# Layer 0's output projection as seven products of half size, on one core

## The chip, the cores and the metric

The kernel runs on one core of one Trainium2 chip. The metric is the device time of one execution in microseconds (us). Before the change the median of three runs is 2584.62 us (2582.84 to 2584.84). One core has TensorE (PE; its weight loads are listed apart as PEld), VectorE (DVE), ScalarE (ACT), GpSimd (POOL) and SyncE (SP), which issues nearly all DMAs of this kernel.

## The reference

One sequence of S = 1024 rows and D = 1024 columns in fp32 goes through two layers. Layer 0 mixes by dilated attention, layer 1 by gated linear attention, and each is followed by a squared-ReLU MLP, with an RMSNorm ahead of every part.

```python
DILATED_GROUPS = ((128, 1), (512, 4), (2048, 16))
for i in range(DEPTH):                     # 2
    h = rmsnorm(x, norm_mix_w[i])
    x = x + (dilated_attention if i % 2 == 0 else gla_mixer)(h, ...)
    h = rmsnorm(x, norm_mlp_w[i])
    x = x + sq_relu_mlp(h, mlp_w_up[i], mlp_w_down[i])
return rmsnorm(x, final_norm_w)
```

The dilated attention has 8 heads of 128 columns and three groups; a group's output is joined with the others by softmax weights. Its last step is `o @ w_out`, a product of 1024 x 1024 by 1024 x 1024, added to x. That step is the subject here.

## The kernel before, in words

**Products in three parts.** A product in fp32 is made of three matmuls in a faster format (fp32r): each operand is split into hi and lo, and hi·hi, hi·lo and lo·hi are summed in PSUM (`mm3`, L195 to L198). A split costs a copy on ScalarE (hi) and a subtraction on VectorE (lo). The large products ahead of the projection are done with seven products of half-size blocks in place of eight (names a11, s1 to s4, a22 and so on, L841); the output projection is not.

**The heads.** The stage that runs from 247 to 855.4 us makes, for 24 pairs (head, group) with number p = 0 to 23, the projection to q, k and v (L841), the rotation (L1309 to L1317), scores, masks, exponentials and the product with v. The three groups come in turn. Classes (L1234 to L1272) is the code of the third group, Attention (L1158 to L1209) that of the other two. The attention of pair p runs while pair p + 1 is projected. The order is written as an agenda: `at(t, fn, rank)` puts a function at step t, a pair has 14 steps, and the functions of one step run by rank. Every engine takes its instructions in the order in which these functions write them. Outputs of the groups go to DRAM (og), and the merge of a head loads them as rows (L1379), weighs them (L1386 to L1395), and joins them into om (L1403, L1404), which goes to DRAM as oscr.

**The projection (the crossing).** `out_proj(0, ...)` (L1713 on) turns rows of the heads' output into columns (`turned.turn`, pT L259; `t_head`, pT L1447), splits them (oTh, oTl, o1h, o1l), splits the rows of w_out (raw, whi, wlo: L133, L152, L153), and makes 8 blocks of 128 rows by 2 halves of the columns by 8 parts of k by 3: 384 matmuls of 128x512 into pd (L196 to L198). The first half of k (heads 0 to 3) is done for all rows first, while the attention of pair 23 and the merge of head 7 still run between; those are the steps of `tail()`, one or two to each `tick()`. Each block is added to x in the tile xs (L1732), and the norm of the MLP (L214 to L242) and its first products follow (pX, pY, L841).

**Buffers and queues.** Tiles come from rings: k4 has slots of 4 KB to a partition and h8 slots of 8 KB. A writer waits for the last reader of the slot that it takes. All the loads and stores of this stage are in SyncE's queue: one that waits (for a buffer or for a result) holds those behind it.

Of the kernel before, what the change touches and what calls it, by code (L numbers as in the profile page):

```python
# [19 lines left out]
P = 128  # L20
# [17 lines left out]
RAW = 4  # L38
# [3 lines left out]
def hybrid_trunk(ctx, tc, x, norm_mix, norm_mlp, norm_fin, a_in, a_out, g_in, g_up, g_b, g_nw,  # L42
# [67 lines left out]

    class Weights:
        def __init__(self):
            self.slots = []
            self.ndma = 0
            self.nprep = 0
            self.used = 0
            self.freed = 0
# [62 lines left out]
    def add_rows(w, k0):  # L180
        for k in range(2):
            W.add(w[P * (k0 + k):P * (k0 + k + 1), :])
# [79 lines left out]
    class Split:  # L262
# [19 lines left out]
    class Halves:  # L282
# [374 lines left out]
    class Trickle:  # L657
# [73 lines left out]

        step = Ahead.step

    def up_columns(i):
        return lambda p, k: [(0, cols(m_up[i], 256 * p, 256, 4 * k, 4))]

# [10 lines left out]
    class Up:  # L747
# [217 lines left out]
    zscr, gscr, uscr = (drp.tile([S, D], F32, name=n) for n in ("zscr", "gscr", "uscr"))  # L965
    wpre = [[[drp.tile([P, 1024], F32, name=f"wp{i}_{p}_{n}") for n in PARTS] for p in range(AHEAD)] for i in range(3)]

    wout = [tuple(drp.tile([P, D], F32, name=f"wo{k}_{n}") for n in range(2)) for k in range(KT)]
    gnw = masks[:, 132:134]

# [430 lines left out]
    def merge_join(rows, eng):  # L1401
        o = t2([P, 4, HD], F32, "om")
        eng.tensor_tensor(o, rows[:, :, 0, 0:HD], rows[:, :, 1, 0:HD], op=OP.add)  # L1403
        eng.tensor_tensor(o, o, rows[:, :, 2, 0:HD], op=OP.add)  # L1404
        return o

    def merge(rows, d, e, z):
        merge_shares(rows, d, e, z)
        o12 = rows.rearrange("p t g c -> p (t g) c")[:, :, 0:HD]
        dve.tensor_tensor(o12, o12, e.rearrange("p t g -> p (t g)").unsqueeze(2).to_broadcast([P, NG * 4, HD]),  # L1410
                          op=OP.mult)
        return merge_join(rows, dve)

    def merges(h, done):

        rows, part = {}, {}

        def load(half):
            rows[half] = merge_load(h, half)

        def start(half):
            part[half] = merge_weights(rows[half])

        def finish(half):
            done(h, half, merge(rows.pop(half), *part.pop(half)))
        return load, start, finish

    oT1 = {}

# [11 lines left out]
    def t_head(h, half, o):  # L1441

        kp, k = divmod(h - 4, 2)
        hi, lo = second(half, kp)
        ps = bank("pT")
        for b in range(4):
            pe.transpose(ps[:, 128 * b:128 * b + 128], o[:, b, :], ident)  # L1447
        split(hi[:, k, :], lo[:, k, :], ps)

    reached = set()  # L1450

    def merged(h, half, o):
        if h < HEADS - 1:
            sp.dma_start(oscr[512 * half:512 * half + 512, HD * h:HD * h + HD].rearrange("(b p) c -> p b c", p=P), o)
        else:
            def last():
                t_head(h, half, o)
                reached.add((0, half))
            at(336 + (28, 34)[half], last)

    def ahead_h8(pairs):

        t = h8([P, 4, 512], F32, "ol")
        sp.dma_start(t, oscr[512 * pairs:512 * pairs + 512, 0:512].rearrange("(b p) c -> p b c", p=P))
        return [t[:, 0:2, :], t[:, 2:4, :]]

    def plan_merges(h, c):

        rows, part = {}, {}

        def load(half):
            rows[half] = merge_load(h, half)

        def weigh(half):
            part[half] = merge_weights(rows[half])

        def join(half):
            del part[half]
            merged(h, half, merge_join(rows.pop(half), dve))
        for half in range(2):  # L1480
            t = c + 9 + 11 * half
            at(t, lambda half=half: load(half))
            if half and h == HEADS - 2:
                t += 9
# [4 lines left out]
            at(t + 10, lambda half=half: join(half), 9)  # L1489


    x0 = []
# [163 lines left out]
    ol = []  # L1656
    turned = Turned(ol, x[0])
    for p in range(heads.count):
        h, g = divmod(p, NG)
        if g == 1 and h:  # L1660
            plan_merges(h - 1, 14 * p)
        if p == heads.count - 1:
            for k in range(0, KT, 2):
                add_rows(a_out, k)
            c = 14 * p
            at(c + 3, lambda: (ol.extend(ahead_h8(0)), W.dma(), W.dma()), 0)
            at(c + 4, lambda: (W.dma(), W.dma()), 0)
            for t in (6, 8, 9, 10):
                at(c + t, lambda: W.prep(dve), 7)
            at(c + 8, lambda: turned.turn(0), 7)  # L1670
            at(c + 9, lambda: (turned.load_x(0), turned.load_x(1)))
            at(c + 11, lambda: turned.turn(1), 7)
        heads.run_head(p)

    def drain_to(mark):
        while mark not in reached:
            steps.popleft()()
            now[0] += 1
            run_due()

    def tail():

        c = clock[0]
        heads.follow(heads.count - 1, c, ((7, 7, 8, 8), (11, 11, 12, 12), (13, 13, 14, 14)))
        ol.extend(ahead_h8(1))
        load, start, finish = merges(HEADS - 1, merged)
        rows = {}

        def early(half):
            t = rows[half] = h8([P, 4, 512], F32, "ol2")  # L1690
            sp.dma_start(t[:, :, 0:384], oscr[512 * half:512 * half + 512, 512:896].rearrange("(b p) c -> p b c", p=P))

        def turn(half, h):
            t_head(h, half, rows[half][:, :, HD * (h - 4):HD * (h - 4) + HD])

        def weights():
            W.early = RAW
        at(c + 1, lambda: early(0))
        at(c + 8, weights)
        at(c + 14, lambda: early(1))  # L1700
        for t, half, h in ((10, 0, 4), (12, 0, 5), (14, 0, 6), (22, 1, 4), (24, 1, 5), (26, 1, 6)):
            at(c + t, lambda half=half, h=h: turn(half, h))
        at(c + 16, lambda: (load(0), load(1)), 9)
        for half, t in ((0, 22), (1, 26)):
            at(c + t, lambda half=half: start(half), 9)
        for half, t in ((0, 24), (1, 28)):
            at(c + t, lambda half=half: finish(half), 9)
        steps.extend([advance] * 44)

    tail()  # L1710


    def out_proj(layer, wbc_row, o, up):  # L1713
# [783 lines left out]
```

## Time and profile before

| what | value |
|---|---|
| median of 3 runs | 2584.62 us (2582.84 to 2584.84) |
| the profiled execution | 2582.79 us, of which the span is 2581.0 |
| granted clock of TensorE | 0.999 |
| DMA moved | 544.33 MB, mean 211 GB/s |

All instants are us from the start of the span. A row of a timeline has start, duration, engine, line, operation, output and inputs, count, and in brackets how long the engine was idle before it and what ended that. In a row by stretches the values are the stretch, its length, busy us (instructions) of PE, PEld, DVE, ACT and POOL, the granted clock, the mean busy share of the 16 DMA engines and GB/s. L numbers are lines of the kernel before, unless said otherwise.

### The profile page before, as it was taken

The numbers are of one execution on the slowest core, as the hardware profiler recorded it, in microseconds if no ns is written. First come the engines' busy times: TensorE is split into PE (matmuls) and PEld (weight loads), VectorE is DVE, ScalarE is ACT, GpSimd is POOL, SyncE is SP. The second block draws the span as 40 slices with busy tenths as digits, with TensorE's granted clock in tenths as the row PEclk, the third lists the DMA queues.
The fourth block names the chain that finished last, engine by engine and source line by source line (L and its number), as shares of the span: only waits on it lengthen the run. The fifth ranks groups of instructions, "written<-read, shape, count | busy, mean of one in ns | idle before, by whom it ended". The sixth has DMA issues, their size and how long they took to land.

```text
span 2581.0 us, 34661 instructions
## 1 busy us (share of the span) xinstructions
PE 2565.0 (99%) x12586; PEld 2120.0 (82%) x12586; DVE 1864.6 (72%) x3000; ACT 1283.6 (50%) x2344; POOL 20.2 (1%) x24
## 2 busy tenths in 40 slices
PE   9999999999999999999999999999999999999998
PEld 6888888888888888888888888888888888888887
DVE  7766788888888766788668795687666666666666
ACT  6443455555545435666544453554335555553344
POOL 0000000000000000000000000110000000000000
PEclk9999999999999999999999999999999999999999
DMA  5785456656565846799798865777445644495543
GB/s 176 243 279 193 108 147 153 157 143 169 141 167 148 270 165 246 263 336 337 265 329 286 288 214 194 271 238 290 171 165 194 237 161 136 147 349 200 189 146 125
DMA packets 357708, 544.33 MB, mean 211 GB/s; under 512 B 25536, under 2 KB 181568, under 8 KB 357536
## 3 DMA queue, kind: packets, MB, share of 16 engines
q1 hardware_dynamic: 357392, 541.85, 64.3%
q8 instruction: 99, 1.62, 0.3%
q14 instruction: 73, 0.60, 0.1%
q10 hardware_dynamic: 144, 0.26, 0.0%
HBM read 338.93 MB, written 177.93 MB: 200 GB/s over the span
## 4 chain that ended last, share of the span: by engine, by line
PE 88%; DVE 4%; ACT 4%; DMA 2%; issue 2%; SPq 0%; DVEq 0%; ACTq 0%
PE pX L841 16%; PE pB L1858 13%; PE pV L841 11%; PE pA L1858 10%; PE pB L1051 8%; PE pA L1051 5%; PE pY L841 5%; PE pZ L841 5%; PE pd L196 2%; PE pd L198 2%; PE pd L197 2%; PE pO L1199 1%; PE pS L1158 1%; PE pT L259 1%; PE pP L1185 1%
## 5 line engine op out<-in xcount | busy, mean ns | idle before, releaser
L1858 PE MATMUL pB<-dh 128*128 128x512 f32 x512 | 199.2, 389 | 0.0
L1858 PE MATMUL pB<-dl,dh 128*128 128x512 f32 x512 | 199.2, 389 | 0.0
L1858 PE MATMUL pB<-dh,dl 128*128 128x512 f32 x512 | 199.2, 389 | 0.0
L205 DVE TENSOR_TENSOR dl<-sin,dh 128x1024 fp32r<-128x1024 f32 x112 | 136.8, 1221 | 62.2 <-ACT dh L202 59.3
L841 PE MATMUL pV<-s4h,wd 128*128 128x512 f32 x480 | 161.4, 398 | 0.6 <-DVE qk L2054 0.4
L202 ACT ACTIVATE dh<-sin 128x1024 fp32r<-128x1024 f32 x112 | 117.8, 1052 | 78.8 <-PE pB L1858 29.8
L1858 PE MATMUL pA<-dh 128*128 128x512 f32 x384 | 149.6, 390 | 0.0
L1858 PE MATMUL pA<-dh,dl 128*128 128x512 f32 x384 | 149.4, 389 | 0.0
L1858 PE MATMUL pA<-dl,dh 128*128 128x512 f32 x384 | 149.4, 389 | 0.0
L846 ACT ACTIVATE e<-pX 128x512 f32<-128x512 f32 x108 | 64.4, 596 | 155.2 <-PE pX L841 155.1
L202 ACT ACTIVATE dh<-kept 128x1024 fp32r<-128x1024 f32 x64 | 67.8, 1060 | 145.1 <-DVE kept L1823 102.0
L779 DVE TENSOR_TENSOR wbl<-t,wbh 128x1024 fp32r<-128x1024 f32 x48 | 58.8, 1226 | 78.7 <-ACT wbh L778 78.7
L1858 PEld LDWEIGHTS pB<-dh,dl 128*128 128x128 f32 x512 | 96.1, 188 | 20.0
L1858 PEld LDWEIGHTS pB<-dh 128*128 128x128 f32 x512 | 96.1, 188 | 20.0
L1858 PEld LDWEIGHTS pB<-dl,dh 128*128 128x128 f32 x512 | 96.1, 188 | 19.8
L841 PEld LDWEIGHTS pV<-s4h,wd 128*128 128x128 f32 x480 | 90.1, 188 | 20.5 <-DVE qk L2054 0.8
L1174 ACT ACTIVATE pt<-pt,orow 128x256 f32<-128x256 f32 (+1 forms) x128 | 59.8, 468 | 91.0 <-DVE orow L1172 87.3
L841 PE MATMUL pX<-s3h,wgh 128*128 128x512 f32 x240 | 96.8, 403 | 0.0
L841 PE MATMUL pX<-s2h,wbh 128*128 128x512 f32 x240 | 96.0, 400 | 0.2
L841 PE MATMUL pV<-s1h,wbh 128*128 128x512 f32 x240 | 95.6, 398 | 0.0
L841 PE MATMUL pY<-a12h,wah 128*128 128x512 f32 x240 | 95.3, 397 | 0.0
L841 PE MATMUL pX<-a11h,wah 128*128 128x512 f32 x240 | 95.0, 396 | 0.0
(370 smaller groups left out, 7251.7 us busy)
## 6 DMA issues: line engine op xcount, KB each, us to landing
sin<-acts SPq DMA_DIRECT2D x112, 512.0 KB, 4.4
acts<-s SPq DMA_DIRECT2D x64, 512.0 KB, 3.5
raw<-in_mlp_w_down_dram SPq DMA_DIRECT2D x64, 512.0 KB, 5.3
raw<-in_attn_w_in_dram SPq DMA_DIRECT2D x96, 256.0 KB, 4.5
cw<-c SPq DMA_DIRECT2D x192, 128.0 KB, 2.3
raw<-in_mlp_w_up_dram SPq DMA_DIRECT2D x48, 512.0 KB, 5.9
acts<-c SPq DMA_DIRECT2D x64, 256.0 KB, 3.0
kept<-in_mlp_w_down_dram SPq DMA_DIRECT2D x32, 512.0 KB, 6.4
```

The lines of the kernel that those rows point to most:

```text
L196: pe.matmul(ps, sh, mh, start=start, stop=False)
L197: pe.matmul(ps, sh, ml, start=False, stop=False)
L198: pe.matmul(ps, sl, mh, start=False, stop=stop)
L202: act.activation(hi, src, AF.Copy)
L205: dve.tensor_tensor(lo, src, hi.bitcast(F32), op=OP.subtract)
L259: pe.transpose(ps[e][:, 64 * n:64 * n + 64], src[k, :], ident[k, k], tile_position=(64 * e, 0))
L779: self.remain(lambda: dve.tensor_tensor(lo, src, hi.bitcast(F32), op=OP.subtract))
L841: pe.matmul(st[b], u[:, k, :], v, start=first and k + n == 0, stop=k == 3 and n == 2, skip_group_check=True)
L846: act.activation(e, self.st[p]["X"], AF.Copy)
L1051: pe.matmul(self.acc[s][t], a[:, c], b[:, k, :], start=fresh and m + k + v == 0, stop=m == 1 and k == 1 and v == 2, skip_group_check=True)
L1174: act.activation(pt[:, i, :128 * n], pt[:, i, :128 * n], AF.Exp, scale=-1.0, bias=m, accum_out=self.row[:, r, HD:HD + 1])
L1858: pe.matmul(self.acc[s][t], a[:, k, c], b[:, k, :], start=fresh and m + k + v == 0, stop=m == 7 and k == 1 and v == 2, skip_group_check=True)
```

## The change

**The products.** The projection of 1024 x 1024 by 1024 x 1024 is cut into blocks of half the size (rows, k and columns in two halves), and done by seven products of 512 x 512 by 512 x 512. The sums of the left operand's blocks are a11, a22, a12, s1 to s4; those of the weights are b11, b21, b22, t1 to t4. There are seven times four blocks (of 128 rows) with four parts of k and three matmuls each. They accumulate in three groups in PSUM: Q (b11, t3, t4), Z (t2, t1, b22), and R (b21). A group is added to xs at one or two places when it holds the right partial sum.

**The weights.** The class `OutParts` makes the weights' sums and splits them beside the heads, in eight plans of four steps each: a plan loads two pieces of w_out (256 KB each), makes four differences of 256 columns, seven splits (three of two pieces together, one of one), and stores hi and lo of the seven in DRAM, in 14 stores of 128 KB. A step runs at t = 7 and t = 14 of a pair, at t = 7 alone if p is a multiple of 3, from p = 1 on, last in its step's rank. All plans are done by p = 20. In pair 23 and the projection they are loaded back: seven sums of four loads, 512 KB each, one load per step of the agenda. The splits of w_out beside the projection (8 on ScalarE, 8 on VectorE) are gone, as are oTl and o1l.

**The agenda.** The sums and splits of the heads' output stand at steps of pair 23 and of `tail()`. The second half of the merge of head 6 is weighed earlier and joined later, straight into the tile that the projection reads.

The core of the diff:

```diff
+        def plan(self, k, cols):
...
+            def cut(i, *names):
...
+                act.activation(hi, src, AF.Copy)
+                def rest():
+                    dve.tensor_tensor(lo, src, hi.bitcast(F32), op=OP.subtract)
+                    for j, name in enumerate(names):
+                        for m, to in enumerate(self.out[name]):
+                            sp.dma_start(to[:, k, cols], both[:, m, j, :].bitcast(F32))
+                self.behind.append(rest)
+            def less(to, a, b):
+                t = r["t"]
+                dve.tensor_tensor(t[:, to, :], t[:, a, :], t[:, b, :], op=OP.subtract)
...
         if p == heads.count - 1:
-            for k in range(0, KT, 2):
-                add_rows(a_out, k)
...
+        elif p:
+            for t in ((7,14), (7,))[p % 3 == 0]:
+                at(14 * p + t, parts.step, 9)
...
+        for t0, name in ((12, "t2"), (18, "t1"), (33, "b22"), (37, "b21")):
+            plan += [(t0 + i, fn) for i, fn in enumerate(proj.load(name))]
...
+        whole("Q", "b11", "a11", True, (1, 0), (1, 1))
+        whole("Q", "t3", "s3", False, (0, 1))
+        for t in range(4):
+            pr.product("Q", "t4", "a22", t, ks)
...
+        whole("Z", "t1", "s1", False, (0, 1))
...
-    out_proj(0, norm_mlp[0], turned, up)
+    project(norm_mlp[0], up)
```

Three places show what it moves. The first is VectorE where pair 12 begins, from the difference of two weight blocks (t, from raw) to the rotation: c is a projected column block, pt the masked scores, cw the swapped half of c. Before:

```order
L815 TENSOR_TENSOR t<-raw 128x512
L816 TENSOR_TENSOR t<-raw,t 128x512
L1300 TENSOR_TENSOR c<-pZ,e_5013 128x512
L1172 ISA pt,orow<-pS,masks 128x128
L1172 ISA orow 128x1
L1172 ISA pt,orow<-pS,masks 128x256
L1172 ISA orow 128x1
L1309 TENSOR_TENSOR cw<-cw,tab 128x512
```

The same place after the change, where wpc is the tile of a split of OutParts:

```order
L954 TENSOR_TENSOR t<-raw 128x512
L955 TENSOR_TENSOR t<-raw,t 128x512
L763 TENSOR_TENSOR wpc<-raw,wpc 128x512
L771 TENSOR_TENSOR raw<-raw 128x256 x2
L1440 TENSOR_TENSOR c<-pZ,e_5157 128x512
L1312 ISA pt,orow<-pS,masks 128x128
L1312 ISA orow 128x1
L1312 ISA pt,orow<-pS,masks 128x256
L1312 ISA orow 128x1
L1449 TENSOR_TENSOR cw<-cw,tab 128x512
```

A split of 512 elements and two differences of 256 stand ahead of the block and of all that follows it in the queue. The second place is VectorE in the crossing, from the last rotation of pair 23 (qT) to the first masks of Classes (pt from pS). Before:

```order
L1317 TENSOR_TENSOR qT<-c,cw 128x16x32
L1732 TENSOR_TENSOR xs<-pd,xs 128x512
L1386 TENSOR_REDUCE mz<-rows 128x4
L1387 TENSOR_TENSOR md<-mz,rows 128x12
L1392 TENSOR_TENSOR md<-me,rows 128x12
L1393 TENSOR_REDUCE mz<-md 128x4
L1394 RECIPROCAL mz<-mz 128x4
L1395 TENSOR_TENSOR me<-me,mz 128x12
L1732 TENSOR_TENSOR xs<-pd,xs 128x512
L1244 ISA pt,orow<-pS,masks 128x64
```

After, where ap are the blocks and sums of the left operand, and s3h and s3l their split:

```order
L871 TENSOR_TENSOR xs<-pQ,xs 128x512 x2
L855 TENSOR_TENSOR ap<-ap 128x4x256
L1449 TENSOR_TENSOR cw<-cw,tab 128x512
L1450 TENSOR_TENSOR c<-c,tab 128x512
L1457 TENSOR_TENSOR qT<-c,cw 128x16x32
L850 TENSOR_TENSOR s3l<-ap,s3h 128x2x256 x2
L871 TENSOR_TENSOR xs<-pQ,xs 128x512 x2
L855 TENSOR_TENSOR ap<-ap 128x4x256
L850 TENSOR_TENSOR s3l<-ap,s3h 128x2x256 x2
L871 TENSOR_TENSOR xs<-pQ,xs 128x512 x2
L1384 ISA pt,orow<-pS,masks 128x64
```

The merge's weights (mz to me) have moved ahead of qT, and sums, splits and adds stand around it. The third place is TensorE where the joined first half of head 7 (om) is turned. Before, after 168 matmuls into pd:

```order
L196 MATMUL pd<-whi,oTh 128x512
L197 MATMUL pd<-wlo,oTh 128x512
L198 MATMUL pd<-whi,oTl 128x512
L1447 MATMUL pT<-ident,om 128x128 x4
L196 MATMUL pd<-whi,oTh 128x512
```

After, in the product of t2 by s2:

```order
L865 MATMUL pZ<-wph,s2h 128x512
L865 MATMUL pZ<-wpl,s2h 128x512
L865 MATMUL pZ<-wph,s2l 128x512
L836 MATMUL pT<-ident,om 128x128 x4
L865 MATMUL pZ<-wph,s2h 128x512
```

The turn of om stands 18 matmuls earlier, after 132 matmuls into pQ and 18 into pZ; the other matmuls between are the same in number.

More of the change, by code (lines that the diff above doesn't have):

```diff
@@ L732, in hybrid_trunk, with __init__, load, one @@
         step = Ahead.step
+    class OutParts:
+        NAMES = ("b11", "t1", "t3", "t2", "b21", "b22", "t4")
+        def __init__(self, w, out):
+            self.w, self.out = w, out
+            self.todo, self.behind = deque(), deque()
+            for k in range(4):
+                for half in range(2):
+                    self.plan(k, slice(256 * half, 256 * half + 256))
+        step = Ahead.step
+        def plan(self, k, cols):
+            r = {}
+            def load():
+                t = r["t"] = k4([P, 4, 256], F32, "raw")
+                for i in range(2):
+                    row = P * (k + 4 * i)
+                    sp.dma_start(t[:, 2 * i:2 * i + 2, :],
+                                 self.w[row:row + P, :].rearrange("p (a c) -> p a c", a=2)[:, :, cols])
+            def cut(i, *names):
+                n = len(names)
+                both = k4([P, 2, 2, 256], F32R, "wpc")
+                hi, lo, src = both[:, 0, :n], both[:, 1, :n], r["t"][:, i:i + n, :]
+                act.activation(hi, src, AF.Copy)
[8 more added lines that the diff above has]
+                dve.tensor_tensor(t[:, to, :], t[:, a, :], t[:, b, :], op=OP.subtract)
+            def one():
+                less(1, 1, 0)
+                cut(0, "b11", "t1")
+            def two():
+                cut(2, "b21", "b22")
+                less(1, 3, 1)
+                less(0, 1, 0)
+            def three():
+                cut(0, "t3", "t2")
+                less(2, 2, 1)
+            def four():
+                cut(2, "t4")
+            if self.todo:
+                last = self.todo.pop()
+                self.todo.append(lambda: (last(), load()))
+            else:
+                self.todo.append(load)
+            self.todo.extend((one, two, three, four))
@@ L1422, in start, with scale @@
             part[half] = merge_weights(rows[half])
+        def scale(half, n):
+            if not n:
+                merge_shares(rows[half], *part[half])
+            merge_scale(rows[half], part[half][1], n)
         def finish(half):
-            done(h, half, merge(rows.pop(half), *part.pop(half)))
-        return load, start, finish
+            r, p = rows.pop(half), part.pop(half)
+            done(h, half, merge_join(r, dve) if half else merge(r, *p))
+        return load, start, finish, scale
     oT1 = {}
@@ L1455, in merged @@
         else:
[L1456 to L1459, printed above, removed]
+            LAST[half] = o
     def ahead_h8(pairs):
@@ L1478, in join @@
             del part[half]
[L1479 removed]
+            if h == HEADS - 2 and half:
+                merge_join(rows.pop(half), dve, LAST["ol"][:, :, 2 * HD:])
+            else:
+                merged(h, half, merge_join(rows.pop(half), dve))
         for half in range(2):
@@ L1679, in drain_to @@
             run_due()
+    while parts.todo or parts.behind:
+        parts.step()
     def tail():
@@ L1693, in turn @@
[L1693 to L1705, printed above, removed]
@@ L1706, in tail, with turn @@
-        for half, t in ((0, 24), (1, 28)):
-            at(c + t, lambda half=half: finish(half), 9)
-        steps.extend([advance] * 44)
-    tail()
+            t = rows[half] = h8([P, 4, 384], F32, "ol2")
+            n = 384 - 128 * half
+            if half:
+                LAST["ol"] = t
+            sp.dma_start(t[:, :, :n], oscr[512 * half:512 * half + 512, 512:512 + n].rearrange("(b p) c -> p b c", p=P))
+        def turn(half, k):
+            proj.head(NAMES[half], k, rows[half][:, :, HD * k:HD * k + HD] if k < 3 else LAST[half])
```

219 lines of the change are left out of this document (196 added, 23 removed).

## The prediction

> **What bounds the kernel now.** I read the page first (part 1, the busy shares; part 4, the chain that ended last), then the busy time by stretches, then the chain and the engines' timelines inside the stretch that the change rewrites.
>
> ```profile
> PE 2565.0 (99%) x12586; PEld 2120.0 (82%) x12586; DVE 1864.6 (72%) x3000; ACT 1283.6 (50%) x2344; POOL 20.2 (1%) x24
> ...
> PE 88%; DVE 4%; ACT 4%; DMA 2%; issue 2%; SPq 0%; DVEq 0%; ACTq 0%
> ```
>
> TensorE is never idle to speak of, and the chain lies on it for 88%: a matmul that goes away is worth its time, as long as nothing else is late behind it. What else could be late is read by stretches (each row: PE, PEld, DVE, ACT, POOL busy, clock, DMA share, GB/s). One row for the heads first; the others run from the end of the last head into the output projection, which starts at 855.4; I call that instant T = 0.
>
> ```profile
> 320.00:855.40 535.40, 534.48 (x3084) 447.07 (x3083) 450.80 (x970) 297.43 (x807) 0.00 (x0) 1.00 0.62 158
> ```
> ```profile
> 833.00:843.00 10.00, 9.80 (x69) 8.19 (x67) 7.44 (x10) 6.15 (x14) 0.00 (x0) 1.00 0.99 310
> 843.00:855.40 12.40, 12.40 (x76) 10.24 (x77) 10.90 (x21) 7.99 (x18) 0.00 (x0) 1.00 1.02 302
> 855.40:869.40 14.00, 14.00 (x77) 11.57 (x77) 11.52 (x26) 4.28 (x14) 0.00 (x0) 1.00 0.89 278
> 869.40:885.00 15.60, 15.60 (x145) 12.85 (x144) 9.07 (x31) 11.96 (x39) 0.00 (x0) 1.00 0.86 253
> 885.00:900.00 15.00, 15.00 (x84) 12.28 (x83) 8.69 (x17) 2.94 (x6) 0.00 (x0) 1.00 0.91 271
> 900.00:915.00 15.00, 14.83 (x69) 11.68 (x68) 13.73 (x22) 3.19 (x5) 0.00 (x0) 1.00 0.11 36
> ```
>
> And from the chain of waits (start, duration, what):
>
> ```profile
> 833.32 7.92 DMA raw<-in_attn_w_out_dram
> ```
>
> Two things count. VectorE is busy for 450.8 of 535.4 us of the heads (84%), so work put beside them meets little slack. And from 833 to 900 the DMA engines are 86 to 102% busy: the last line is a load of output weights that is itself on the chain. The change adds to both.
>
> **The matmuls that go.** Two groups of twelve 128x512 matmuls on the chain:
>
> ```profile
> 958.63 2.72 PE pX L841 x12
> 961.35 2.72 PE pY L841 x12
> ```
>
> 2.72 / 12 = 0.227 us each (the groups' mean of 389 ns overlaps the next matmul). 384 of them become 28 x 12 = 336: 48 x 0.227 = **-10.9 us**. The splits of the weights that held TensorE between 900 and 915 go too: 15.00 - 14.83 = **-0.2**. The clock is 1.00 in every row; I keep it.
>
> **The crossing: the waits that come.** The profile shows none of the new waits; I bound them by counting what stands in the queues. First VectorE ahead of Classes' scores (the last head's third group):
>
> ```profile
> 866.85 1.04 DVE L1317 TENSOR_TENSOR qT<-c,cw 128x512 f32<-128x512 f32 x1
> ...
> 868.42 0.15 DVE L1386 TENSOR_REDUCE mz<-rows 128x4 f32<-128x12 f32 x1
> ...
> 869.70 0.17 DVE L1395 TENSOR_TENSOR me<-me,mz 128x12 f32<-128x12 f32 x1
> ...
> 875.44 0.22 DVE L1244 CUSTOM_DVE_ANT_0 pt<-pS,masks 128x64 f32<-128x64 f32 x1
> ```
> ```profile
> 869.41 1.08 PE pS L1234 x32
> ...
> 877.30 0.44 PE pP L1254 x4
> ```
>
> Before, qT was done at T = 12.5 and its scores came at 14.0. The next rows price one VectorE instruction by the start of the next one: 1.14 us for 1024 elements (559.46 to 560.60), 0.6 for 512 (561.20 to 561.79).
>
> ```profile
> 559.46 1.21 DVE L779 TENSOR_TENSOR wgl<-t,wgh 128x1024 fp32r<-128x1024 f32 x1
> 560.60 0.68 DVE L1300 TENSOR_TENSOR c<-pY,e 128x512 f32<-128x512 f32 x1
> 561.20 0.68 DVE L1309 TENSOR_TENSOR cw<-cw,tab 128x512 f32<-128x512 f32 x1
> 561.79 0.68 DVE L1310 TENSOR_TENSOR c<-c,tab 128x512 f32<-128x512 f32 x1
> 562.51 1.12 DVE L1317 TENSOR_TENSOR qT<-c,cw 128x512 f32<-128x512 f32 x1
> ```
>
> In the new order two more adds into xs (1.2), one sum of 1024 elements (1.1) and the merge weights that stood behind it (868.42 to 869.87, 1.4) come ahead of qT: 12.5 + 3.7 = 16.2. TensorE gets there with four or five products more, at 14.9: 1.3 late. Behind qT, up to the second batch of masks, stand 2 s3 splits of two (2.4), two pairs of adds (2.4), another sum (1.1), two batches of masks (1.2) and an add (0.6): 7.7, so 23.9, and with the exponentials on ScalarE some 25.4, where TensorE wants pP 7.4 us after the scores (their own 1.1, two products of 2.72, two transposes of 0.44), at 16.2 + 7.4 = 23.6: 1.8 more late, and with the wake-ups between engines I take 3.3 for both.
>
> This delay goes on into the merge of the last head, which the next rows time:
>
> ```profile
> 890.01 0.93 SPq L1379 DMA_DIRECT2D rows<-og x2
> ```
> ```profile
> 896.05 0.17 DVE L1386 TENSOR_REDUCE mz<-rows 128x4 f32<-128x12 f32 x1
> ...
> 900.05 1.76 DVE L1410 TENSOR_TENSOR rows<-rows,me 128x1536 f32<-128x1536 f32 x1
> ...
> 902.58 0.69 DVE L1404 TENSOR_TENSOR om<-om,rows 128x512 f32<-128x512 f32 x1
> ```
> ```profile
> 903.75 0.60 PE L1447 MATMUL pT<-ident,om 128*128 128x128 f32 x4
> ```
>
> Rows are issued at 890.01 and used at 896.05 (6.1 later); from there to om are 7.2 us, of which some 2.5 are other work of VectorE between: 4.7. Before, the transposes of om stood 168 products in, at 903.75, with om ready at 903.27. Now they stand 150 products in: 48.35 - 18 x 0.227 = T 44.3. With Classes 3.3 later om is ready at 896.05 + 3.3 + 4.7 = 904.05, T 48.7: 4.4 us late, which includes the 3.3. That is the floor of this term.
>
> The other end is the DMA queue. Ahead of Classes' og stand from 832.8 on, by the sizes in SyncE's program: 14 loads of operands at 0.52 MB (7.3), eight of x (4.2), the heads' blocks (2.1 and 1.3), rows (0.8), v (1.05), cw (1.05), og and oscr (1.3): 19.1 MB, and og itself 0.5; before, the stretches moved 14.7 MB from 833 to 885 (10 x 310 + 12.4 x 302 + 14 x 278 + 15.6 x 253). At the 0.31 MB/us of the saturated row 833:843 the 19.6 MB end at 832.8 + 63.2 = 896.0; SyncE waits for og to land before it issues rows, so 896.0 + 6.1 + 4.7 = 906.8, T 51.4: 7.1 late. The floor needs 0.325 or more. I take 6.0, between the two and nearer the rate that this stretch itself shows: **+6.0**.
>
> [...]
>
> **The crossing's end.** The norm of the first pair of blocks:
>
> ```profile
> 921.90 0.69 DVE L1732 TENSOR_TENSOR xs<-pd,xs 128x512 f32<-128x512 f32 x1 [2.03 <-PE pd L198]
> ...
> 925.17 2.74 DVE L242 SCALAR_TENSOR_TENSOR xn<-xs,y,wbc 128x512 f32<-128x512 f32 x4
> ```
>
> From the last add to the end of xn are 6.0 us. Now two more adds and a split of s4 (1.8), with its copy on ScalarE (0.6), come into that chain, 8.4, and TensorE has three products (two of 2.72, one of 2.04: 7.5) until it turns these blocks: **+0.9**, between 0 and 2.
>
> **The heads.** The steps of OutParts put 0.3 to 1.3 us of VectorE work ahead of a rope at the end of each of 14 heads, and as much in the middle of 20. It decides where TensorE waits for qT right after: heads whose successor starts Classes. Such a pair (qT and the scores) at 411, 562 (its qT is quoted above) and 790:
>
> ```profile
> 411.20 1.06 DVE L1317 TENSOR_TENSOR qT<-c,cw 128x512 f32<-128x512 f32 x1
> ```
> ```profile
> 412.60 1.15 PE L1234 MATMUL pS<-kT,qT 128*64 128x64 f32 x32
> ```
> ```profile
> 563.99 1.15 PE L1234 MATMUL pS<-kT,qT 128*64 128x64 f32 x32
> ```
> ```profile
> 790.55 1.11 DVE L1317 TENSOR_TENSOR qT<-c,cw 128x512 f32<-128x512 f32 x1
> ```
> ```profile
> 791.72 1.15 PE L1234 MATMUL pS<-kT,qT 128*64 128x64 f32 x32
> ```
>
> qT is ready 0.34, 0.36 and 0.06 us early. In front of it now come a split (0.6), a split and two sums (0.6 + 2 x 0.34), one sum (0.34): late by 0.26, 0.92 and 0.28. No row shows 256 elements; its price lies between half of 0.6 and 0.6, and I take 0.34, near the half, since 1024 cost 1.14 where twice 512 are 1.2. Six such heads, counted alike, give **+2.9**. Elsewhere in the heads VectorE pauses for ScalarE before its next use, and I cost the steps at nothing; without that cover, 33 steps at up to 0.9 us. The 112 stores (14.7 MB) and 16 loads (4.2 MB) add 18.9 MB to the heads' 535.4 x 0.158 = 85 MB; at a share of 0.62 I cost them at nothing, and SyncE's issues with them.
>
> [...]
>
> **The sum.** -10.9 - 0.2 + 6.0 + 0.9 + 2.9 = -1.3 us. The profiled execution took 2582.79 (span 2581.0); with the change 2581.5. The median of the runs is 1.83 above it: 2584.62 - 1.3 = **2583.3**.
>
> **Rivals.** First what the page's slices of 64.5 us show the DMA engines to have moved elsewhere:
>
> ```profile
> GB/s 176 243 279 193 108 147 153 157 143 169 141 167 148 270 165 246 263 336 337 265 329 286 288 214 194 271 238 290 171 165 194 237 161 136 147 349 200 189 146 125
> ```
>
> (a) The waits are small (chance 0.38). The queue drains at 0.325 MB/us or better, so the crossing loses its floor of 4.4, and the heads and the crossing's end hide their steps, since VectorE has 84 us of idle time in the heads: -10.9 - 0.2 + 4.4 = -6.7, **2577.9**. For it: the page's busier slices reach 336 to 349 GB/s in other stages. Against it: the slack of 0.06 to 0.36 above, with no pause of VectorE between the step and qT.
>
> (b) Slower: the DMA queue ahead of the rows of the last head (0.20). If the stretch drains at the 0.262 MB/us of 869 to 900 (mean of 253 and 271) and not at 0.31, the 19.6 MB end at 832.8 + 74.8 = 907.6, om is ready at 918.4, T 63.0, 18.7 late, and cw, which feeds the ropes, is late in the same queue: -10.9 - 0.2 + 18.7 + 0.9 + 2.9 = +11.4, **2596.0**. It turns slower by more than 5.2 us when the term passes 12.5, at a rate under 0.286. Against it: those two rows were not saturated (0.86 and 0.91).
>
> My forecast, part of the gain eaten by both, has 0.42. That the products don't shrink is no rival: the program has 336.
>
> **Chances and range.** 0.2% of 2584.6, what a measurement of this kernel can tell from no change, is 5.2 us: faster means under 2579.4, slower over 2589.8. So faster 0.38, no difference 0.42, slower 0.20. The forecast's own range is 2580 to 2587 (queue at 0.325 to 0.295, heads between 1 and 3); the range that holds 8 in 10 takes in rival (a) with its end at -8.6 (2576.0) and the nearer part of (b), 2590.5.
>
> **What would show it.** Right: TensorE waits of 4 to 8 us in all between T = 14 and T = 50, ended by VectorE's qT, by pt, and by om; a DMA share near 1 from 833 to 897; six waits of 0.2 to 1 us at Classes' scores in the heads. Wrong: PE idle under 2 us in the crossing (then rival a); PE waiting on operands wph or wpl, on cw, or over 12 us before om's transposes (rival b); waits in most of the heads, above all for buffers that SyncE's loads wait for, which I cost at nothing.

## The result and the profile after

The changed kernel takes 2597.49 us (median of 6 runs, 2592.72 to 2600.98) against 2583.26 before (6 runs, 2582.47 to 2584.84): a ratio of 1.0054, with an interval of 1.0041 to 1.0067. It is slower by 14.2 us. The profiled execution took 2596.60 us, with a span of 2594.4 where before had 2581.0. The six runs of the change spread over 8.3 us, those of before over 2.4, and a profile shows one execution, so a difference of a microsecond or two between two profiles can be chance.

To find where the 13.4 us of the spans came from, I set the same three instants side by side: the first matmul of the projection, the first of the next stage that reads dh, and the end. From PE's timeline, before and then after:

```profile
855.42 0.47 PE L196 MATMUL pd<-whi,oTh 128*128 128x512 f32 x1
...
1265.43 0.39 PE L1858 MATMUL pB<-dh 128*128 128x512 f32 x1
```
```profile
868.58 0.47 PE L865 MATMUL pQ<-wph,a11h 128*128 128x512 f32 x1
...
1279.38 0.39 PE L2136 MATMUL pB<-dh 128*128 128x512 f32 x1
```

The projection starts 13.2 us later, and all of that is lost after the first scores of the heads (283.5 before, 283.3 after). From there to dh are 410.0 us before and 410.8 after. The rest is alike. So there are two losses: the heads (from their first scores to the projection) lose 13.2 us, and the projection and what follows lose the whole gain of 10.9 us.

The waits of TensorE in the heads, before (320 to 855) and after (320 to 868): line, what was waited for, us in all, times, the longest.

```profile
PE pO L1265 <- ACT pt L1255: 0.5, 2, 0.3
PE pS L1234 <- DVE qT L1317: 0.2, 1, 0.2
PE pV L841 <- ACT e L1337: 0.2, 1, 0.2
```
```profile
PE pS L1374 <- DVE qT L1457: 4.3, 6, 1.0
PE pO L1339 <- ACT pt L1327: 4.1, 9, 0.6
PE pO L1405 <- ACT pt L1395: 0.5, 2, 0.3
PE pP L1394 <- ACT pt L1386: 0.3, 1, 0.3
```

The first row after is the one that I had forecast, with its count of six. The second was not in my sum. In this list, before and after, a wait is the idle time of the engine. It holds a part of the loss only, since a late weight load (PEld) counts apart (PEld waits 9.1 us at pO and 6.8 at the scores there); measured from one matmul's start to the next, against the usual distance of the same pair of instructions, distances over 0.2 us too long add up to 7.3 us at pO, 4.7 at pS and 0.5 at pP.

The stretches of the projection after (same columns as before):

```profile
843.00:855.00 12.00, 12.00 (x72) 10.46 (x71) 10.37 (x14) 8.47 (x22) 0.00 (x0) 1.00 0.98 290
855.00:870.00 15.00, 15.00 (x102) 12.29 (x101) 7.90 (x19) 8.87 (x22) 0.00 (x0) 1.00 1.07 365
870.00:885.00 15.00, 11.54 (x83) 8.95 (x82) 9.75 (x22) 5.37 (x15) 0.00 (x0) 0.99 1.04 306
885.00:900.00 15.00, 15.00 (x95) 12.40 (x95) 11.90 (x32) 10.54 (x35) 0.00 (x0) 0.89 1.10 315
900.00:915.00 15.00, 15.00 (x102) 12.25 (x102) 13.44 (x26) 8.36 (x15) 0.00 (x0) 1.00 0.82 263
915.00:930.00 15.00, 12.83 (x52) 10.09 (x51) 8.47 (x13) 3.76 (x7) 0.00 (x0) 0.89 0.77 295
```

The DMA engines are at a share of 0.98 to 1.10 for 57 us, and TensorE, which was idle for 0.17 us in the projection's stretches before, is idle for 3.5 and 2.2 us in two stretches. Its granted clock is 0.89 in two of them. The chain of waits shows the way there:

```profile
861.54 9.41 DMA xs<-in_x_dram
870.96 9.07 DMA cw<-c
...
880.13 0.69 DVE cw L1449
...
883.08 0.18 DVE me L1535
...
883.29 0.99 ACT rows L1539 x3
884.28 0.38 ACT pt L1327
...
884.70 1.55 PE pO L1339 x6
...
909.93 8.72 DMA wpl<-wqt
...
918.69 4.38 PE pZ L865 x11
```

VectorE has made the block c at 866.1 (it starts at 865.45 and lasts 0.69). SyncE, with the loads ahead of it, issues the two cw pieces of c at 869.73 and 870.96, the second when a load of x lands (861.54 + 9.41), and this piece of 128 KB, which takes 2.4 us at the median of this run, takes 9.07. VectorE waits for it and holds the merge weights (me) that stand behind the rotation; ScalarE waits for me, with the copy of pt behind that in its queue; and pO, which needs that copy, comes 2.0 us late. The lo part of t2 takes 8.72 and holds pZ for 2.2 us.

### The profile page after: what moved, and what is told of

Its sections match the earlier page's. It is cut to its first block, busy times and chain, and to the rows that moved or that the text cites. A ratio compares the mean times of both kernels' runs of the same rounds, so it can differ in the third digit from the quotient of the medians.

```text
span 2594.4 us, 34910 instructions
## 1 busy us (share of the span) xinstructions
PE 2564.3 (99%) x12538; PEld 2114.2 (81%) x12538; DVE 1899.0 (73%) x3076; ACT 1310.3 (51%) x2403; POOL 20.2 (1%) x24
## 4 chain that ended last, share of the span: by engine, by line
PE 63%; DVE 3%; DMA 3%; ACT 1%; issue 1%; SPq 0%; DVEq 0%; ACTq 0%
PE pB L2136 13%; PE pX L980 11%; PE pA L2136 10%; PE pV L980 7%; PE pY L980 4%; PE pZ L980 3%; PE pB L1191 3%; PE pA L1191 3%; PE pd L194 1%; PE pd L196 1%; PE pd L195 1%; PE pQ L865 1%; PE pT L257 1%; PE pZ L865 1%; DMA rows<-og 1%
```

## The experiments

Each kernel is compared with the kernel before, run on the same chip beside it (medians 2583.26 to 2584.25). The table gives the difference of the medians and two numbers of each profiled execution: when the projection starts, and the time from there to dh.

| kernel | us | over before | projection starts | from there to dh |
|---|---|---|---|---|
| before | 2583.26 | 0 | 855.4 | 410.0 |
| the change | 2597.49 | +14.2 | 868.6 | 410.8 |
| e1 no arithmetic in the steps | 2588.42 | +4.5 | 859.9 | 410.9 |
| e2 no stores | 2590.09 | +6.2 | 864.7 | 406.9 |
| e3 half the loads | 2592.09 | +8.2 | 869.3 | 404.9 |
| e4 before, with the steps | 2598.51 | +14.6 | 872.6 | 410.1 |
| e5 no copies on ScalarE | 2597.70 | +13.9 | 870.1 | 411.8 |
| e6 loads by GpSimd | 2609.78 | +26.0 | 877.6 | 413.7 |
| e7 steps at 7 and 11 | 2594.41 | +10.6 | 866.2 | 410.6 |
| e8 OutParts on GpSimd | 2623.05 | +39.2 | 883.3 | 422.2 |
| e9 steps ahead of the heads | 2609.85 | +25.6 | 883.9 | 408.4 |
| e10 the same, x earlier | 2625.04 | +40.8 | 896.0 | 412.9 |
| e11 e9 with four loads of 28 | 2608.22 | +24.0 | 884.6 | 407.2 |
| e12 the change with four loads of 28 | 2588.58 | +4.9 | 868.7 | 404.4 |
| e13 before, 48 matmuls left out | 2574.62 | -9.1 | 855.0 | 401.4 |

My theory after the result was this: the heads lose to the steps' instructions in the queues of VectorE and ScalarE, the projection to the DMA queue. The rivals were that the heads lose to the stores and SyncE's queue, and the projection to the order of VectorE's work.

**e1, the steps without arithmetic.**

```diff
-                act.activation(hi, src, AF.Copy)
-                    dve.tensor_tensor(lo, src, hi.bitcast(F32), op=OP.subtract)
...
-                            sp.dma_start(to[:, k, cols], both[:, m, j, :].bitcast(F32))
+                            sp.dma_start(to[:, k, cols], src[:, j, :])
...
-                dve.tensor_tensor(t[:, to, :], t[:, a, :], t[:, b, :], op=OP.subtract)
+                return
```

> The changed kernel, in which OutParts does no arithmetic beside the heads: its raw pieces are loaded and stored as before (the same 112 stores and 16 loads), and the copies, splits and differences are left out, so the operands hold unsplit weights. Theory 1 (the heads lose some 13 us to the steps' instructions in the queues of VectorE and ScalarE): 2585 us, 2583 to 2588, and the span up to the first projection matmul is back within 2 us of the kernel before. Theory 2 (the heads lose it to the stores and SyncE's queue, which make cw and the weights' loads late): 2595 to 2598, hardly less than the changed kernel.

Measured: 4.5 us over before, 9.7 better than the change (of the differences to before, here and below). The heads lose 4.4 us in place of 13.2, more than the 2 that I allowed, and the waits that are left are small:

```profile
PE pO L1336 <- ACT pt L1324: 1.2, 2, 0.6
PE pP L1391 <- ACT pt L1383: 0.7, 1, 0.7
PE pS L1371 <- DVE qT L1454: 0.6, 3, 0.3
```

Arithmetic is 8.7 of the 13.2 us (868.6 - 859.9). The projection is unchanged at 410.9.

**e2, the arithmetic without the stores.** The lines that store are gone, and the projection loads other scratch:

```diff
-                    for j, name in enumerate(names):
-                        for m, to in enumerate(self.out[name]):
-                            sp.dma_start(to[:, k, cols], both[:, m, j, :].bitcast(F32))
...
-                sp.dma_start(t.bitcast(F32), self.dram[name][m][:, 2 * j:2 * j + 2, :])
+                src = wpre[0][2 * j + m][OutParts.NAMES.index(name)]
+                sp.dma_start(t.bitcast(F32), src.rearrange("p (a c) -> p a c", a=2))
```

> The changed kernel with all of OutParts' arithmetic but none of its 112 stores; the projection's 28 loads of the same size read other scratch in DRAM instead, so the operands are not w_out's. Theory 1 (queues of VectorE and ScalarE): 2596 us, 2594 to 2599, as the changed kernel. Theory 2 (stores and SyncE's queue): 2584 to 2587.

Measured: 6.2 us over before; neither theory had that. The heads lose 9.3, so the stores are 3.9 of the 13.2, and the wait at Classes' scores stays:

```profile
PE pS L1372 <- DVE qT L1455: 4.2, 6, 1.0
PE pO L1337 <- ACT pt L1325: 2.4, 6, 0.6
```

With e1 the two parts add up: 8.7 for the arithmetic and 3.9 for the stores, 0.5 for the rest. What the list shows of the stores' part is at pO, whose waits fall from 4.1 to 2.4 us. The projection is 3.9 us shorter too: the wait for t2's lo part goes from 2.17 to 0.37 us there, and the slow matmuls behind it (see the last section) are gone; the mean clock of the profiled execution is 0.999 and not 0.998. Why that load lands sooner is not settled.

**e3, half the bytes in the projection.**

```diff
-                t = (w.hi, w.lo)[m][j] = k4([P, 2, 512], F32R, ("wph", "wpl")[m])
+                if m:
+                    w.lo[j] = w.hi[j]
+                    return
+                t = w.hi[j] = k4([P, 2, 512], F32R, "wph")
```

> The changed kernel without the 14 loads of the weights' lo parts in the projection (7.3 MB less): the hi tile stands in for lo, so the product's low digits are off; TensorE, VectorE and ScalarE do the same work. Theory 1 for the projection (the DMA queue makes cw, og, rows and the lo part of t2 late, and TensorE runs at a lower clock after the waits): 7 us faster than the changed kernel, 2588 to 2592, and no wait on cw. Theory 3 (VectorE's order in the projection makes Classes late, whatever the DMA does): 2596 to 2598, with the waits before Classes' scores still there.

Measured: 8.2 us over before, 6.0 better than the change, with 404.9 from the projection's start to dh (5.9 less). The waits for cw fall from 3.4 to 1.1 us, and pO's two waits, which lasted 1.46 and 2.00, last 0.90 and 0.42. The granted clock is 1.00 in all stretches from 843 to 930. A wait on cw is left, which Theory 1 did not have.

**e4, the steps alone in the kernel before.** OutParts, its scratch and the lines that put its steps into the agenda are added to before:

```diff
+        elif p:
+            for t in ((7,14), (7,))[p % 3 == 0]:
+                at(14 * p + t, parts.step, 9)
```

> The kernel before with OutParts and its steps added beside the heads (sums, splits and stores that nobody reads) and the old projection. Theory 1: the heads alone cost 13 us, so 2596, 2594 to 2598. If the heads' loss needs the rest of the change (the new head 23, the merge moved): 2584 to 2588.

Measured: 14.6 us over before, with the old projection unchanged at 410.1. The steps cost the heads 17.1 us in the profiled execution, the slowest of four and 1.6 us over their median, so some 15 us in the median. That is not much more than in the change; what the change saves beside them (the splits of w_out in pair 23, the merge's new place) was not tried apart.

**e5, which engine's arithmetic.** ScalarE's copies are left out, VectorE's work is not:

```diff
-                act.activation(hi, src, AF.Copy)
...
-                    dve.tensor_tensor(lo, src, hi.bitcast(F32), op=OP.subtract)
+                    dve.tensor_tensor(lo, src, src, op=OP.subtract)
```

> The changed kernel without OutParts' copies on ScalarE (the split subtracts the raw piece from itself and both stores take that, so the operands are not w_out's); VectorE's instructions, loads and stores are as in the changed kernel. If the heads' loss comes through VectorE (steps ahead of qT and of the masks, behind which ScalarE's exponentials and TensorE wait): 2595 to 2598, and the six waits at Classes' scores stay at 4.7 us in all. If it is ScalarE's copies ahead of pt: 2588 to 2591, and the waits of pO go from 7 us to under 3.

Measured: 2597.70, as the change, and its waits in the heads too:

```profile
PE pO L1337 <- ACT pt L1325: 5.4, 12, 0.8
PE pS L1372 <- DVE qT L1455: 4.8, 6, 1.0
```

ScalarE's copies cost nothing that shows, though it is ScalarE that pO waits for. The timelines show what lies ahead of one such wait (VectorE, ScalarE, then TensorE, of the change):

```profile
785.57 0.17 DVE L1526 TENSOR_REDUCE mz<-rows 128x4 f32<-128x12 f32 x1 [1.62 <-DMA rows<-og]
...
790.56 0.69 DVE L1440 TENSOR_TENSOR c<-pX,e 128x512 f32<-128x512 f32 x1 [0.51 <-ACT e L1477]
791.17 0.28 DVE L1312 CUSTOM_DVE_ANT_0 pt<-pS,masks 128x128 f32<-128x128 f32 x1
791.38 0.42 DVE L1312 CUSTOM_DVE_ANT_0 pt<-pS,masks 128x256 f32<-128x256 f32 x1
```
```profile
791.55 0.40 ACT L1314 ACTIVATE pt<-pt,orow 128x128 f32<-128x128 f32 x1 [1.02 <-DVE orow L1312]
...
791.96 0.50 ACT L1314 ACTIVATE pt<-pt,orow 128x256 f32<-128x256 f32 x1
...
792.45 0.97 ACT L1539 ACTIVATE rows<-rows,me 128x128 f32<-128x128 f32 x3
793.32 0.47 ACT L1327 ACTIVATE pt<-pP 128x384 f32<-128x384 f32 x1
```
```profile
793.85 0.82 PE L1339 MATMUL pO<-v,pt 128*128 128x128 f32 x5 [0.62 <-ACT pt L1327]
```

The same place in the kernel before:

```profile
772.44 0.17 DVE L1386 TENSOR_REDUCE mz<-rows 128x4 f32<-128x12 f32 x1 [0.48 <-DMA rows<-og]
...
777.37 0.69 DVE L1300 TENSOR_TENSOR c<-pX,e 128x512 f32<-128x512 f32 x1 [0.50 <-ACT e L1337]
```
```profile
778.37 0.40 ACT L1174 ACTIVATE pt<-pt,orow 128x128 f32<-128x128 f32 x1 [1.02 <-DVE orow L1172]
...
780.14 0.47 ACT L1187 ACTIVATE pt<-pP 128x384 f32<-128x384 f32 x1
```
```profile
780.93 0.83 PE L1199 MATMUL pO<-v,pt 128*128 128x128 f32 x6
```

ScalarE is idle for 1.02 us until VectorE has masked; then the exponentials, three scalings of the merge and the copy follow without a gap. From c to the copy this takes 2.8 us in both kernels, and before, pO finds the copy done. So the delay does not arise in these rows. It is there 5 us earlier, where VectorE waits 1.62 us for the rows of the merge and not 0.48; what follows in its queue, and in ScalarE's behind it, comes later, and pO waits. Six of the change's eight waits for rows come 8.2 to 8.3 us ahead of a late pO. In e1 the waits for rows are as long in all (9.0 us and 8.9), and two of ten are followed so. That fits a VectorE which without the arithmetic has the time to catch up; it was not tried apart, and why the rows come later was not either.

**e6, the projection's loads in another queue.** `sp.dma_start` becomes `pool.dma_start` in `Project.load`.

> The changed kernel with the projection's 28 loads of the weights' sums issued by GpSimd and not by SyncE; everything else stays, the bytes too. If the projection loses its gain to the order in one queue (cw, og and rows stand behind the loads): cw is no longer waited for there, and 2590 to 2593. If it is the bytes themselves (the DMA engines are full): 2596 to 2600.

Measured: 26.0 over before, worse than either expectation. Out of SyncE's order the loads start earlier, and the stretches 855:870, 870:885 and 885:900 stand at a share of 1.08, 1.02 and 1.05; VectorE waits 8.7 us for cw and 10.2 us for rows. Of the 8.7, however, 8.2 lie ahead of the projection, where the first loads now start 38 us before it and not 22; in the projection itself cw costs 0.5 us, as the first expectation had it, and TensorE's longest wait there is 8.6 us for om, behind the rows. So the one queue had kept the loads back, and this run does not separate its order from the bytes.

**e7, the steps at other places.** `((7,14), (7,))[p % 3 == 0]` becomes `(7, 11)`.

> The changed kernel with OutParts' steps at t = 7 and t = 11 of every pair in place of 7 and 14: at 11 a step stands ahead of the split wbl, where VectorE waits for ScalarE's copy wbh for some 1.5 us in each pair. If the loss in the heads is the place of VectorE's work: the waits at Classes' scores go from 4.7 to under 1 us, and 2588 to 2592. If any place costs the same, since VectorE and the loads are short of time throughout: 2595 to 2599.

Measured: 10.6 over before, 3.6 better than the change, between the two expectations. The waits at Classes' scores go, as expected, but those of pO grow:

```profile
PE pO L1339 <- ACT pt L1327: 6.4, 9, 1.4
PE pS L1374 <- DVE qT L1457: 0.8, 4, 0.2
```

The place decides which wait the work turns into, and little of how much: the heads lose 10.8 us in place of 13.2. With two steps in every pair the plans are also done some three pairs earlier, so the run changes more than the place.

**e8, OutParts on GpSimd.** Its `act`, `dve` and `sp` become `pool`, and so do the projection's loads.

> The changed kernel with all of OutParts on GpSimd: its copies, splits and differences, its loads and stores, and the 28 loads of the projection too. If VectorE's queue and SyncE's queue are what the heads lose by: the heads are back within 3 us of the kernel before and the time is 2577 to 2586. If GpSimd's arithmetic takes VectorE's access to SBUF or its DMAs are slow, so that its weights come late: over 2595.

Measured: 39.2 over before. OutParts' 32 splits (24 of 128x512, 8 of 128x256) take GpSimd 1.53 us in the mean where they take VectorE 0.62 in the change, and the waits at Classes' scores rise to 8.8 us (from start to start). The stores land in 4.8 and 4.5 us at the median (into wqt and wqb), SyncE's in the change in 3.9 and 3.6. Whether its arithmetic or its DMAs make the loss was not tried apart, and that it takes VectorE's access to SBUF was not shown.

**e9 and e10, the steps ahead of the heads.** In the loop over the values' products, one step to each from the ninth on; in e10 the loads of x come from four steps before pair 23 on, apart from those of the weights.

```diff
         if n >= 9:
             ahead.step()
+            parts.step()
...
-            for t in ((7,14), (7,))[p % 3 == 0]:
+            for t in (11,):
```

> The changed kernel with OutParts' steps in the stage ahead of the heads (one per product of the values from the ninth on, the last two at t = 11 of the first pairs), where VectorE is 63 to 67% busy: 31 of its 32 splits stand there. If the heads lost their 13 us to VectorE's work at 84% busy: the heads come back to within 2 us of the kernel before, the earlier stage loses 0 to 2, and the time is 2584 to 2588, since the projection still loses what it gains. If the steps cost the same wherever they stand: 2594 to 2599.

> As e9_vals, with the eight loads of x (4.2 MB) issued from four steps before the last head on, and the weights' loads from its second step on, each earlier by up to six steps. If the bytes from 833 to 900 are what the projection waits for: 3 to 6 us faster than e9_vals, 2579 to 2584. If the order of VectorE's work is: as e9_vals within 1 us.

Measured: 25.6 and 40.8 over before; I was wrong on both. In e9 the heads are back indeed (571.3 us from their first scores to the projection, 571.9 before), but the stage ahead of them is 29 us longer: VectorE had room there, and the DMA engines are at a share of 0.99 and 0.92 with the steps.

```profile
160.00:200.00 40.00, 35.09 (x139) 26.60 (x138) 31.59 (x45) 18.95 (x29) 0.00 (x0) 0.91 0.99 336
200.00:240.00 40.00, 36.41 (x160) 29.52 (x159) 23.81 (x35) 13.68 (x22) 0.00 (x0) 1.00 0.92 326
```

Before, these stretches had shares of 0.84 and 0.60, and TensorE was busy for all of both. What TensorE waits for there is c, which VectorE and ScalarE write; VectorE waits 8.6 us for OutParts' own loads of w_out between 120 and 284, and SyncE 16.6 us for its splits before it can store them. Which of these makes the 29 us was not tried apart. In e10 an earlier load of x also waits 11.4 us for its buffer in the heads, with others behind it.

**e11 and e12, four loads of 28.** All seven sums take b11's tiles. In e11, on top of e9, the other loads leave no step (`return []`), so those of x move up; in e12, on the change itself, they leave empty steps, so every other load keeps its place. The line of e12:

```diff
+            if name != "b11":
+                self.w[name] = self.w["b11"]
+                return [lambda: None] * 4
```

> As e9_vals, with the four loads of b11 standing in for all seven sums of the weights (24 loads, 12.6 MB less; the product is not w_out's). If the loads are what the projection waits for: 410.8 us from its first matmul to the next stage become 401 to 404, and the time is 7 to 10 us under e9_vals, 2575 to 2579. If VectorE's order holds it (my floor of 4.4 and more): 406 or more, less than 5 us under e9_vals.

> The changed kernel with b11's four loads standing in for all seven sums, as in e11, but on the changed kernel's own heads and with every other load, those of x too, at its old step. If the bytes ahead of cw and of the rows of the last head are what the projection waits for: no wait for cw over 0.5 us, and 402 to 404 us from its first matmul to the next stage in place of 410.8, so 2588 to 2591. If VectorE's order is: 407 or more, over 2593.

Measured: e11 wins 1.2 us from the projection's start to dh against e9, which spoke against the bytes. But there all eight loads of x had moved up ahead of the cw pieces with which the chain above begins; SyncE issued them 4.1 and 5.4 us after c was started, as late as in the change (4.3 and 5.5). In e12 they had not, and the two pieces are issued 0.7 and 1.2 us after it: 404.4 against 410.8, 6.4 us less, and the median is 9.3 lower in its difference to before (its profiled execution, at 2590.22, lies 1.6 over its median). VectorE waits for cw once, for 1.2 us, more than the 0.5 expected. Once issued, the two pieces take as long as in the change (9.3 us against 9.9 and 9.1). So what makes them late is what stands ahead of them in SyncE's queue, be it weights or x.

**e13, the price of the matmuls.** In the kernel before, 48 of the 384 matmuls take no part:

```diff
+                short = not layer and (k == 1 or (k == 3 and tb < 4) or (k == 2 and tb + n == 0))
-                mm3(ps, a, b, wh[:, 512 * n:512 * n + 512], wl[:, 512 * n:512 * n + 512], k == 0, k == 3)
+                (mm2 if short else mm3)(ps, a, b, wh[:, 512 * n:512 * n + 512], wl[:, 512 * n:512 * n + 512], k == 0, k == 3)
```

> The kernel before with 48 of the 384 matmuls of layer 0's output projection left out (the hi-lo product for some parts of k, so the low digits are off), all else as it is. If TensorE bounds the projection: 10.9 us less, 2572 to 2574. If something else is late there at once: over 2576.

Measured: 9.1 us faster (ratio 0.9965, 0.9952 to 0.9978), 8.6 of them between the projection's start and dh. TensorE gets to Classes earlier and waits there:

```profile
PE pP L1258 <- ACT pt L1250: 1.6, 2, 1.3
PE pS L1238 <- DVE qT L1321: 0.3, 1, 0.3
```

With these 1.9 us the 8.6 are 10.5, so the matmuls are worth about what I counted; some 2 us of it turn into waits at once, without any of the change's loads and splits.

## Why the prediction was wrong, point by point

**The matmuls** (-10.9): right. e13 gives 9.1 with waits of some 2 us behind it.

**The waits in the crossing** (+6.0, and +0.9 at its end): the step that waits come there was right; their path was in part another, and the size was too small. With 410.0 - 10.9 - 0.2 = 398.9 us as what it would take without waits, the change has 11.9 us of them, against 6.9 in the sum. I had TensorE wait for qT, for pt and for om. In the change it waits for neither qT nor om there. It waits for pt at pO of Attention (L1339; 1.46 and 2.00), the second time because cw is late, and for t2's lo part (2.17), which was my sign of rival (b); only the end, with 0.6 and 0.3, is as forecast. e12, with most loads gone, leaves 404.4 - 398.9 = 5.5 us, near the 5.3 of my floor and end, but that is luck: its waits are at pO (1.0), at pP (0.7) and at the end, and none is for om, from which the floor was worked out. The difference to it, 6.4 us, is the DMA queue, and close to half of that is the clock, which I had kept at 1.00: some 2.9 us, worked out in the last section. I had taken the rate at 0.31 MB/us and thought of og and rows. The stretch 855 to 870 reached 0.365, over the 0.325 that the floor needs, and still cw and t2's lo part were late: the rate alone did not decide it, and what e12 takes away is loads that SyncE had ahead of them. I had named cw in rival (b) and not priced it.

**The heads** (+2.9, measured 13.2): the step that failed. The sentence that VectorE pauses elsewhere in the heads, so that the other steps cost nothing, was wrong, and so was the cost of nothing for the stores. With e1 and e2 the arithmetic is 8.7 us and the stores are 3.9. TensorE pays at two places, from start to start: 4.7 us at the six Classes' scores and 7.3 at pO. The second I had at nothing, and it holds parts of both: the waits there, 4.1 us in the list of the change, are 1.2 without the arithmetic (e1) and 2.4 without the stores (e2), so the 7.3 and the 3.9 do not add.

The wait for qT at the six heads was there, at 4.7 us in place of 2.9. My price for 256 elements is not the reason. The split lasts 0.42 us, but the next instruction starts 0.34 us after it, and the sum was made from start to start:

```profile
792.92 0.42 DVE L763 TENSOR_TENSOR wpc<-raw,wpc 128x256 fp32r<-128x256 f32 x1
793.26 0.69 DVE L1440 TENSOR_TENSOR c<-pZ,e 128x512 f32<-128x512 f32 x1
```

One reason is the slack of 0.06 us that I read at 790: in all six waits of the change the scores start 0.05 or 0.06 us after qT is done, so there was none. Another is that VectorE came to these heads late already. At the first of them (414.61 in the change) qT is 0.75 us late where I had 0.26, and VectorE had waited 1.40 us for rows at 394.69, with no such wait before. How the stores work is open: the wait of the merge for its rows is 8.9 us in the change and 9.0 in e1, where it was 1.1 before, but it is still 6.1 in e2 without them.

**The rivals.** Rival (b) gave 2596.0 with a loss of 18.7 us in the DMA queue of the crossing alone. The time is near, the account is not: that queue cost 6.4 us, and more than half of the loss came from the heads, which no rival of mine held. Rival (a) failed with its condition, that the heads hide their steps.

No kernel here that computes the whole beats the one before. The nearest was e7, at 10.6 us over it.

## What to carry to other kernels

Where an engine is 84% busy and works in order, price a step by what stands behind it in its queue and by the engines that wait for that, and not by the idle time of the stretch: here 27 us of small steps (VectorE is busy 474.7 us in the heads of the change and 447.8 in those of e1) became 8.7 us of TensorE's time, at places that never wait for them directly. For work that is moved into DRAM and back, read the share of the DMA engines in the stretches where it goes out and comes in; where they stood near a share of 1 here (0.98 to 1.10), loads ahead in the same queue made a transfer of 128 KB late that someone waited for (issued 5.5 us after c was started, and 1.2 in e12). Taking matmuls away from a chain that is all TensorE paid here (9.1 us in e13), but the next engine's lead over it is to be read first.

## What the runs showed of the hardware

After some long waits TensorE runs slower for a few matmuls. The change has two such waits in the projection, and from PE's timeline behind the second:

```profile
918.69 0.58 PE L865 MATMUL pZ<-wpl,s2h 128*128 128x512 f32 x1 [2.17 <-DMA wpl<-wqt]
919.07 0.63 PE L865 MATMUL pZ<-wph,s2l 128*128 128x512 f32 x1
919.50 0.63 PE L865 MATMUL pZ<-wph,s2h 128*128 128x512 f32 x1
...
922.44 0.39 PE L865 MATMUL pZ<-wpl,s2h 128*128 128x512 f32 x1
922.67 0.40 PE L865 MATMUL pZ<-wph,s2l 128*128 128x512 f32 x1
```

Starts are 0.43 us apart and not 0.23, until 922.4: nine matmuls take 3.75 us and not 2.1, some 1.7 us on top of a wait of 2.17, and the granted clock is 0.51 from 918.9 to 922.4 (0.89 in the stretch from 915 to 930). Behind the first wait (2.00 us, to 884.70) six matmuls from 885.91 take 2.54 us and not 1.4, some 1.2 us more, so 2.9 in all, and the clock is 0.51 from 884.8 to 888.3. After the wait of 1.46 us at 879.0 it does not happen (starts are 0.23 us apart from 880.0 on), and not after every longer one: in e10 TensorE waits 2.06 us for t2's lo part at 949.41 and 2.77 us at 218.85, and the matmuls behind both start 0.23 us apart; in e9 the stretch 200:240 (its row above) has 3.6 us of idle time in all at a granted clock of 1.00. What decides is not shown.

A queue of its own did not keep small transfers quick: with the loads on GpSimd's queue (e6) the cw pieces on SyncE's still took 5.6 to 11.0 us around the projection's start (2.4 at the median of the run), and VectorE waited for them three times, 8.7 us in all. GpSimd took 1.53 us in the mean for OutParts' splits and VectorE 0.62 (e8, the change).

The matmuls on fp32r tiles were the faster ones: 128x512 start 0.227 us apart, and on fp32 tiles 128x256 start 0.22 apart (scores of the kernel before, L1158, at 311.25 and 311.47).
